# A two-layer SSD / RG-LRU trunk on one core: the order of the instructions taken from the scheduler's timeline model instead of its default model

## The chip, the cores and the metric

One core of a Trainium2 chip. The time is device microseconds (us) of one execution of the program. Five engines are spoken of: PE multiplies matrices, DVE and ACT work on vectors, POOL does so more slowly and reduces across partitions, SP issues loads and stores. Each engine runs its own list of instructions strictly in the order in which the compiled program has them, and waits at an instruction until what it needs is there.

## The reference

A step of a trunk of two layers runs over a new prompt (16 meta tokens and 1024 tokens) and over 8 running sequences of one new token each. All of it is float32:

```
for i in range(2):
    h = rms_norm(x, norm_mix_pre[i])
    m = ssd_mixer(h, ...) if i == 0 else rglru_mixer(h, ...)
    x = x + rms_norm(m, norm_mix_post[i])
    h = rms_norm(x, norm_ffn_pre[i])
    x = x + rms_norm(sq_relu_mlp(h, ffn_w1[i], ffn_w2[i]), norm_ffn_post[i])
```

The SSD mixer projects 1024 features to 6176, convolves over 4 tokens, and in chunks of 128 tokens computes for each of 8 groups of heads `scores = (C B^T) * L`, `y = scores x + (C h) * exp(cs)` and `h = h * exp(cs_end) + B^T (x * decay)`. The RG-LRU mixer has a gate, a convolution and a linear recurrence over the tokens. The MLP is `relu(x w1)^2 w2` with 4096 hidden features. Outputs are the new rows and the states of both mixers, for the prompt and for the running sequences.

## The kernel before

**Matrices.** Weights come in strips of 128 x 2048 float32, one MB each (`load_strip`, tile `ws`). A strip is scaled by a power of two and split in two float16 parts (`wconv`, `split`; tiles `wh` and, for the form with sums, `wp`), and every product is done in three passes of those parts. The power of two needs the largest magnitude of the strip: DVE or ACT takes it for each partition (`rm`), POOL's `partition_all_reduce` takes it over partitions (`wgb`, L265), and DVE works out the factors from `wgb` (`qw`, `pw`, `sw`, `winv`, in `strip_scale` and `pow2`). Where a `partition_all_reduce` stands among POOL's other work, the compiled program has a further POOL instruction (shown as `ISA` without operands) ahead of it and one behind it.

**Order of the program.** The mixer of layer 0 runs first (SSD: 8 groups, `ssd_group`), then its MLP (`ffn(0)`), then the RG-LRU mixer (`lru`) and `ffn(1)`. The source is written as lanes: generators that go one step on each `tick()`. Conversions of coming strips, sums of operands and normalisations are lanes beside the products. Beside the steps of an SSD group run the projections of the next one (`fill`).

**SSD group.** For each of 9 chunks PE transposes (`tp`) and multiplies (`cb`, `st`, `yo`); DVE forms `L`, `cbm`, `xdt`, `xdd`; the state is carried by POOL (`hst <- hst * ecd`, L1060) and then DVE (`hst <- hst + st`, L1061). Once per group POOL multiplies the 8 states of the running sequences (`h <- h * decfm`, 128 x 2048).

**MLP.** `ffn` goes through four blocks of 1024 hidden features. In blocks 1 to 3, and in the second products of blocks 0 to 2, the products are done as `unit`: seven products of quarters instead of eight, three units for a strip (the tokens lie in three chunks). A unit takes four of the eight PSUM tiles; ACT and DVE add its products up (`z`, `acc`). PE can therefore be at most two units ahead of DVE. A strip of these products needs, beside `wh`, the split quarters (`wp`, DVE's second part) and then four sums of quarters that POOL forms in the room of the strip (`ws <- ws`, in `sums`); only then does the next strip's `partition_all_reduce` come on POOL. Strips for w1 are called H strips here, those for w2 S strips. Ahead of block 1, POOL also forms the sums of the input (`input_sums`, tiles `f`).

**What sets the order.** Instructions go through `Queue` (L78), so almost all of them carry its lines: L89, or L92 where one has been pinned behind the one before. `hold` pins all engines to program order for the start of the kernel; activations that need a table stay in program order (`tab`). Everything else is put in order by the scheduler of the tile framework within what the data, the tiles' rooms and these pins allow. Its model of the machine is what `kernel()` gives to `TileContext` (L1655).

Of the kernel before, what the change touches and what calls it, by code (L numbers as in the profile page):

```python
# [17 lines left out]
DRAM = bass.MemoryType.DRAM  # L18
# [3 lines left out]
P = 128  # L22
D = 1024
KT = 8
# [3 lines left out]
T = 1050  # L28
# [25 lines left out]
def cols(c):  # L54
    """The columns of a chunk of tokens."""
    return slice(c * CW, c * CW + WC[c])


class Carve:
    """Small float32 tiles cut from larger ones."""  # L60
# [17 lines left out]
class Queue:  # L78
    """An engine; while hold is set its instructions are issued in program order, and later ones behind them."""
# [38 lines left out]
class Body:  # L118
# [7 lines left out]
    # ------------------------------------------------------- order of work  # L126
    def tick(self):
        """One step of every piece of work that runs beside the matrix products."""
        for lane in list(self.lanes):
            if next(lane, self) is self:  # L130
                self.lanes.remove(lane)
# [5 lines left out]
    def tab(self, *args, **kw):  # L137
        """An activation whose function needs a table set: these stay in program order."""
        if self.last_tab is None or self.nc.scalar.hold:
            self.last_tab = self.nc.scalar.activation(*args, **kw)  # L140
        else:
            with self.tc.issue_after(self.last_tab.ins):
                self.last_tab = self.nc.scalar.activation(*args, **kw)
# [8 lines left out]
    # ---------------------------------------------------------------- setup  # L152
    def setup(self):
# [8 lines left out]
        c = self.const  # L162
# [19 lines left out]
        # pre-norm gains and group-norm gains scaled by a power of two so that hi/lo fit float16  # L182
# [13 lines left out]
        # the inputs of the ffn leave room for sums of four  # L196
# [48 lines left out]
    def pow2(self, b, n, pool, tag):  # L245
        """p = the power of two at or below b; s = 2^14 / p."""
        nc = self.nc
        q = pool.tile([P, n], F32, tag="q" + tag, name="q" + tag)
        nc.vector.tensor_scalar(q, b, 1e-25, 1e25, op0=OP.max, op1=OP.min)
        p = pool.tile([P, n], F32, tag="p" + tag, name="p" + tag)  # L250
        nc.vector.tensor_scalar(p.bitcast(I32), q.bitcast(I32), EXPMASK, None, op0=OP.bitwise_and)
        s = pool.tile([P, n], F32, tag="s" + tag, name="s" + tag)
        nc.vector.tensor_scalar(s.bitcast(I32), p.bitcast(I32), -1.0, POW2SUM, op0=OP.mult, op1=OP.add)
        return s, p

    # -------------------------------------------------------------- weights
# [14 lines left out]
    def split(self, w, st, s, parts):  # L271
        """w = float16 hi and lo parts of st * s, s [P, parts] by contiguous column ranges."""
# [12 lines left out]
    def wconv(self, st, kind, cols=SW):  # L285
        """A strip of weights as float16 hi and lo parts [P, 2, KT, cols], the factor that undoes its scaling and,
        for kinds h and H, the factor of its hidden units. Kind a takes a bound from the sums of the magnitudes, kind s
        one that kind g found before; kinds 2 and S carry the factors of the hidden rows. Kinds H and S are for the
        products by Winograd's form: with the quarters that are used as they are."""
# [50 lines left out]
    def quarter(self, s, inv):  # L340
        """Scales that leave room for sums of four."""
# [7 lines left out]
    def sums(self, wp, st, s, npair, parts):  # L349
        """Steps: the quarters of a strip [K tiles, M] that are used as they are, A11, A12, A22 (A ij: m tile i, k  # L350
        tiles of parity j), as float16 parts in wp; then the sums of Winograd's form in the room of the strip. Only
        the first npair pairs of k tiles."""
# [20 lines left out]
    def product(self, ps, i, w, B, T, npair):  # L373
        """ps = one of the seven products of quarters over the first pairs of k tiles, three passes of the float16
        parts; open for the products of the other pairs where there are any."""
# [14 lines left out]
    def quadrant(self, w, B, npair, i, l):  # L390
        """The operands of m tile i by half l of the tokens over the other pairs."""
# [26 lines left out]
    def hidden_scale(self, wmax, inv):  # L418
        """The factors of one strip's hidden units: t = 2^7, or 2^6 where the squares are summed, / (power of two at or
        below the bound on the values before the square, the norm of the input times that of a column); returns  # L420
        t / (scales of the product); 1 / t^2 goes to rj."""
# [21 lines left out]
    def summed(self, b, s):  # L443
        """Whether the hidden units of a strip of block b enter the second product by Winograd's form."""
        return b < 3 and s < NSUM
# [6 lines left out]
    def bundle(self, ps, w, m, act, c, kts=range(KT), first=True, last=True):  # L452
        """ps += sum over k of w[k, m tile]^T act[k, chunk c], three passes of the float16 parts."""
# [14 lines left out]
    def new_u(self):  # L468
        """Float16 parts of the normed input by chunk and k tile."""
# [4 lines left out]
    def u_rows(self, U, c):  # L474
        """The bytes of chunk c of U as float32 rows."""
        return U[:, c].bitcast(F32).rearrange("p k s c -> p k (s c)")

    # ---------------------------------------------------------------- norms
    def rstd(self, sumsq, n, pool, w):
        """1 / sqrt(mean + eps) on every partition, from per-partition sums of squares."""  # L480
# [17 lines left out]
    def normed(self, x, ss, i, hi, lo, pool):  # L498
        """Steps: the pre-norm i of a chunk (its k tiles in x), as float16 parts in hi and lo [P, KT, n]."""
# [15 lines left out]
    def boundary(self, m, ss, xc, piece, ipost, xdst, ipre, U, pool):  # L515
        """Steps: x + norm(m) for a piece of a chunk to xdst; then its pre-norm."""
# [37 lines left out]
    def last_phase(self, ws, act, ipost, xsrc, xdst, ipre, evac, pre=None, split0=None):  # L554
        """The last product before a norm, chunk by chunk; the norms of a chunk run beside the next one."""
# [47 lines left out]
    def first_phase(self, strips, act, evac):  # L603
        """Products of the first strips after a norm: chunk 2 of the input comes last."""
# [15 lines left out]
    # ------------------------------------------------------------------ SSD  # L620
# [67 lines left out]
    def start_x(self, c):  # L688
        """A chunk of the input, in the room of later rows: its k tiles, and room left over."""
# [25 lines left out]
    def start_norm(self, U, c, x, sq, ufs):  # L715
        """Steps: the first pre-norm of a chunk."""
# [29 lines left out]
    def start(self, U):  # L746
        """The first pre-norm beside the first products, issued in this order."""
# [20 lines left out]
    def dt_phase(self, U, dts, dtt, w):  # L768
        """Step sizes, decays and their cumulative sums, tokens on partitions: columns (tile, head); tiles 0-7
        are the chunks of the prompt, 8 the meta tokens, 9 the sample tokens."""  # L770
# [31 lines left out]
        # the sums again, tokens along the rows, in DRAM, from where they are spread over the partitions  # L802
# [22 lines left out]
        # sample tokens  # L825
# [3 lines left out]
        # head rows by sample, then spread over the partitions of the features  # L829
# [13 lines left out]
    def softplus(self, out, x, pool, n, parts=1):  # L843
        """max(x, 0) + log1p(exp(-|x|)), the logarithm by the series of 2 artanh(e / (2 + e)); by parts of the
        columns that don't wait for each other."""
# [23 lines left out]
    def evac_ext(self, pre, ps, c, inv, bias=0.0):  # L869
        """A chunk of projected columns into the layout of the convolution: 8 x (3 state + 1), 3 zeros, tokens."""  # L870
# [10 lines left out]
    def conv_tile(self, pre, out, w4, b1, cvo):  # L881
        """Depthwise convolution of width 4; the last three columns of each sequence go to cvo [P, 27]."""
# [16 lines left out]
    def proj_x(self, g, start=False):  # L899
        """Projection and convolution of the x, B and C columns of a group."""  # L900
# [84 lines left out]
    def ssd_group(self, g):  # L985
# [26 lines left out]
        def spread(i):  # L1012
            """The cumulative sums of a chunk's tokens on every partition."""
# [68 lines left out]
        def sample_bc():  # L1082
            """B and C of the sample tokens, by way of DRAM, on every partition."""
# [22 lines left out]
        def sample_b(b2):  # L1106
            """Two sample tokens: h += x B and y = h C, B and C spread over the partitions."""
# [45 lines left out]
    def group_norm(self, g):  # L1153
        """Steps: gate, norm within the group, float16 parts."""
# [25 lines left out]
    def half_a(self):  # L1180
        """The first half of the output projection, kept in DRAM by chunks."""
# [43 lines left out]
    # ------------------------------------------------------------------ FFN  # L1225
    def ffn(self, l):
# [8 lines left out]
        for b in range(4):  # L1235
# [3 lines left out]
            def square(c, s, r):  # L1239
                """The squares of r (m tile, half of the tokens) as float16 parts, and their sums."""  # L1240
# [78 lines left out]
    def t_sums(self, f, t1, t234):  # L1319
        """Steps: the sums of quarters of the right operand for Winograd's form, in their room in f (B jl: k tiles of  # L1320
        parity j, half l of a chunk's tokens, the last half first): T1 = B12 - B11, T2 = B22 - T1, T3 = B22 - B12,
        T4 = B21 - T2, and their float16 parts."""
# [9 lines left out]
    def input_sums(self, U, TT, fp):  # L1332
        """Steps: the sums of quarters of the input, T1 in the room of B12 and the others in TT."""
# [16 lines left out]
    def unit(self, w, BT, c, npair, fp):  # L1350
        """Two m tiles by a chunk, [C12, C11, C22, C21] (C il: m tile i, half l of the tokens, the last half first), the
        first pairs of k tiles by Winograd's form: seven products of quarters."""
# [27 lines left out]
    # ------------------------------------------------------------------ LRU  # L1380
    def lru(self):
# [99 lines left out]
        # a bound on |h gate|: (32.3 max|x| + max|h0|) (norm of u times that of a column of weights + max|b|)  # L1481
# [74 lines left out]
def _strips(w, ns):  # L1556
    """[K, N] as [ns, 128, (K / 128) * (N / ns)], each strip contiguous per partition."""
# [4 lines left out]
def _fm(x):  # L1562
    """[..., n * 128] as [128, n, ...]"""
# [95 lines left out]
```

## Time and profile before

| | |
|---|---|
| runs of the kernel before | 2834.26, 2834.31 and 2837.87 us, median 2834.31 |
| span of the profiled execution | 2836.7 us |
| PE busy | 2583.1 us, 91% of the span |
| DVE, ACT, POOL busy | 2110.1, 1322.6, 691.4 us |
| instructions | 56933 |

No time beside its span is listed for the profiled execution; the span lies 2.4 us above the median of the runs and 1.2 us below the slowest.

The stages by the clock of the profile: the start to 71 us, the SSD groups to 852, the end of the mixer to 1065, the MLP of layer 0 to 1704, a boundary to 1846, the gates of the RG-LRU to 1988, its output to 2130, the MLP of layer 1 to 2769, the end to 2837. In a row of the timeline the first number is the start, the second the duration; the bracket at the end tells how long the engine had been idle and what ended that. Durations of neighbouring rows overlap by some 0.08 us, so that sums are taken from starts where that matters. "issue" in a bracket means that the engine waited for nothing that the profile shows.

### The profile page before, as it was taken

What the parts mean: (1) busy time and instruction counts of PE and PEld (TensorE: products, weight loads), DVE (VectorE), ACT (ScalarE), POOL (GpSimd) and SP (SyncE); (2) the same over time, 40 slices, a digit from 0 to 9 for tenths busy, and PEclk for the clock granted to TensorE, in tenths of its full rate; (3) what the DMA queues carried; (4) which work ended last, traced back from release to release, by engine and by line L of the source; (5) the groups of instructions that cost most, each with busy time, mean ns of one, the idle gap of its engine ahead of it and who ended that gap; (6) DMA issues with size and microseconds to landing.
All of it is one profiled execution on the core that took longest, in us unless ns stands there. A gap on an engine that the chain in (4) does not pass through costs nothing. (4 is left out here: it accounts for less than half of the span.)

```text
span 2836.7 us, 56933 instructions
## 1 busy us (share of the span) xinstructions
PE 2583.1 (91%) x23209; PEld 2060.6 (73%) x23209; DVE 2110.1 (74%) x5043; ACT 1322.6 (47%) x2148; POOL 691.4 (24%) x972
## 2 busy tenths in 40 slices
PE   4999999999999999789989999979999779989998
PEld 2666666666666667789989976646667779989976
DVE  4889778977873685568778788787685667878776
ACT  4655455545544354344253344658564335253352
POOL 2222111212212024442232201123014452231301
PEclk9999999999999999889999999989999989999999
DMA  3232233223345320101122123110220101111122
GB/s 123 99 119 90 87 107 115 102 88 108 113 159 187 117 106 31 46 31 46 61 72 79 46 110 113 63 62 33 89 108 31 46 31 46 47 45 53 54 73 95
DMA packets 52758, 229.15 MB, mean 81 GB/s; under 512 B 9056, under 2 KB 18416, under 8 KB 31632
## 3 DMA queue, kind: packets, MB, share of 16 engines
q1 hardware_dynamic: 46112, 190.81, 19.1%
q0 software_dynamic: 6384, 34.71, 3.1%
q8 instruction: 181, 2.97, 0.4%
q14 instruction: 81, 0.66, 0.1%
HBM read 186.28 MB, written 39.22 MB: 79 GB/s over the span
## 5 line engine op out<-in xcount | busy, mean ns | idle before, releaser
L89 PEld LDWEIGHTS <-wh 128*128 128x128 f16 x17040 | 1504.0, 99 | 503.7 <-issue 54.7
L89 PE MATMUL mm<-U,wh 128*128 128x350 f16 (+3 forms) x7056 | 989.4, 297 | 20.7 <-ACT rr L89 13.2
L89 PE MATMUL mm<-H,wh 128*128 128x175 f16 (+5 forms) x5664 | 557.7, 253 | 35.3 <-DVE z L89 30.4
L89 PEld LDWEIGHTS <-wp 128*128 128x128 f16 x3888 | 311.0, 99 | 87.6 <-issue 60.5
L89 POOL TENSOR_TENSOR ws<-ws 128x256 f32<-128x256 f32 (+1 forms) x192 | 205.2, 1069 | 328.6 <-DVE wp L89 214.4
L89 DVE TENSOR_TENSOR z<-z,mm 128x175 f32<-128x175 f32 (+3 forms) x648 | 228.4, 370 | 29.2 <-ACT z L89 22.0
L89 POOL PARTITION_ALL_REDUCE wgb<-rm x100 | 55.5, 555 | 656.6 <-issue 338.4
L89 PE MATMUL mm<-U,wp 128*128 128x175 f16 (+1 forms) x1728 | 154.8, 245 | 55.2 <-DVE z L89 55.1
L89 PE MATMUL mm<-TT,wh 128*128 128x175 f16 (+1 forms) x1728 | 167.0, 248 | 10.2 <-ACT TT L89 9.3
L89 ACT ACTIVATE z<-z,ti 128x700 f32<-128x700 f32 (+1 forms) x72 | 63.0, 875 | 183.5 <-DVE z L89 183.5
L89 DVE SCALAR_TENSOR_TENSOR wh<-ws,sw,wh 128x1024 f16<-128x1024 f32 x94 | 122.0, 1320 | 28.3 <-ACT wh L89 28.3
L89 DVE TENSOR_SCALAR qw<-wgb 128x1 f32<-128x1 f32 x103 | 15.5, 150 | 167.3 <-POOL wgb L89 167.1
L89 DVE SCALAR_TENSOR_TENSOR wh<-ws,s,wh 128x256 f16<-128x256 f32 x256 | 114.7, 490 | 11.1 <-ACT wh L89 11.1
L89 DVE TENSOR_REDUCE rm<-ws 128x1 f32<-128x2048 f32 x40 | 91.3, 2281 | 31.2 <-DMA ws<-w 26.7
L89 PE MATMUL mm<-H,wp 128*128 128x175 f16 (+1 forms) x864 | 90.5, 241 | 25.5 <-DVE z L89 23.1
L89 DVE TENSOR_TENSOR ss<-ss,sqt 128x350 f32<-128x350 f32 (+3 forms) x154 | 75.9, 500 | 41.8 <-ACT sqt L89 41.1
L89 ACT ACTIVATE wh<-ws,s 128x512 f16<-128x512 f32 x128 | 83.0, 710 | 48.0 <-POOL ws L89 23.2
L89 DVE SCALAR_TENSOR_TENSOR conv<-pre,ssmall,conv 128x1072 f32<-128x1072 f32 x78 | 103.8, 1330 | 0.1
L89 ACT ACTIVATE wh<-ws,sw 128x2048 f16<-128x2048 f32 x47 | 93.7, 1993 | 14.5 <-DVE sw L89 11.7
L89 DVE TENSOR_SCALAR L<-L,ncs 128x128 f32<-128x128 f32 (+1 forms) x288 | 90.6, 357 | 13.2 <-DMA L<-csd 13.2
L89 DVE TENSOR_TENSOR H<-z,H 128x175 f16<-128x175 f32 (+5 forms) x120 | 81.2, 694 | 23.6 <-ACT H L89 19.5
L89 ACT ACTIVATE pre<-mm,undo 128x8 f32<-128x8 f32 (+1 forms) x104 | 46.5, 474 | 110.7 <-PE mm L89 110.7
(279 smaller groups left out, 4176.9 us busy)
## 6 DMA issues: line engine op xcount, KB each, us to landing
ws<-w SPq DMA_DIRECT2D x64, 1024.0 KB, 4.9
ws<-w_ssd_in SPq DMA_DIRECT2D x24, 1024.0 KB, 5.4
L<-csd SPq DMA_DIRECT2D x64, 256.0 KB, 3.2
ws<-w_lru_in SPq DMA_DIRECT2D x12, 1024.0 KB, 4.9
xd<-xc POOLq DMA_DIRECT2D x6, 1400.0 KB, 5.5
xc<-xd SPq DMA_DIRECT2D x6, 1400.0 KB, 6.0
h<-ssd_h SPq DMA_DIRECT2D x8, 1024.0 KB, 4.9
bc<-bcd SPq DMA_DIRECT2D x8, 1024.0 KB, 4.8
```

Of the source, the lines that this page charges most:

```text
L89: r = f(*args, **kw)
```

## The change

One argument in `kernel()`; the rest of the diff takes comments and docstrings out, and no line number moves.

```
-    with _tile.TileContext(nc) as tc:
+    with _tile.TileContext(nc, schedule_with_timeline_sim=True) as tc:
         tile_trunk(tc, aps)
```

The scheduler puts the same instructions in another order. The counts on PE, DVE, ACT and SP are those of before; POOL has four of the operand-less `ISA` instructions fewer. PE's order is as before in the units of both MLPs; in the SSD groups projections of the next group stand ahead of steps that they stood behind. DVE's order differs by 30 to 100 places in the SSD groups and by three or four in the MLPs. Three places follow.

**Place 1, an H strip of the MLP.** DVE's rows between the last split of one strip (`wp_15764`) and the factors of the next one (`qw_16198`, from POOL's `wgb_16196`), in the kernel before:

```order
L89 SCALAR_TENSOR_TENSOR wp_15764<-ws_15397,sq4_15880,wp_15764 128x512
L89 TENSOR_TENSOR z_15368<-z_15368,mm_15367 128x175 x2
L89 SCALAR_TENSOR_TENSOR acc_10692<-z_15368,iq4_15229,acc_10692 128x700
L89 TENSOR_TENSOR z_15482<-z_15482,mm_15478 128x175
L89 TENSOR_REDUCE rm_16147<-ws_15761 128x1
L89 TENSOR_TENSOR z_15482<-mm_15479,z_15482 128x2x175
L89 TENSOR_TENSOR z_15482<-z_15482,mm_15479 128x175
L89 TENSOR_TENSOR z_15482<-z_15482,mm_15480 128x2x175
L89 TENSOR_TENSOR z_15482<-z_15482,mm_15481 128x175 x2
L89 SCALAR_TENSOR_TENSOR acc_10692<-z_15482,iq4_15229,acc_10692 128x700
L89 TENSOR_TENSOR z_15607<-z_15607,mm_15603 128x174
L89 TENSOR_SCALAR qw_16198<-wgb_16196 128x1
```

and in the changed kernel:

```order
L89 SCALAR_TENSOR_TENSOR wp_15764<-ws_15397,sq4_15880,wp_15764 128x512 x3
L89 TENSOR_TENSOR z_15368<-z_15368,mm_15364 128x175
L89 TENSOR_TENSOR z_15368<-mm_15365,z_15368 128x2x175
L89 TENSOR_TENSOR z_15368<-z_15368,mm_15365 128x175
L89 TENSOR_TENSOR z_15368<-z_15368,mm_15367 128x175
L89 TENSOR_REDUCE rm_16147<-ws_15761 128x1
L89 TENSOR_TENSOR z_15368<-z_15368,mm_15366 128x2x175
L89 TENSOR_TENSOR z_15368<-z_15368,mm_15367 128x175
L89 TENSOR_TENSOR z_15482<-z_15482,mm_15478 128x175
L89 TENSOR_SCALAR qw_16198<-wgb_16196 128x1
L89 TENSOR_SCALAR lb_16443<-wgb_16196,gb_103 128x1
L89 SCALAR_TENSOR_TENSOR acc_10692<-z_15368,iq4_15229,acc_10692 128x700
```

In the kernel before all of `z_15482`, the first row of `z_15607` and both `acc` rows stand ahead of `qw`; in the changed kernel only the seven rows of `z_15368` and `z_15482` that are shown and `rm` do, and both `acc` rows come behind it. The same place on POOL, before:

```order
L89 TENSOR_TENSOR ws_15397<-ws_15397 128x4x128 x4
L89 ISA
L89 ISA wgb_16196<-rm_16147 128x1
L89 ISA
L89 TENSOR_TENSOR ws_15761<-ws_15761 128x4x128 x4
```

and after:

```order
L89 TENSOR_TENSOR ws_15397<-ws_15397 128x4x128 x3
L89 ISA
L89 ISA wgb_16196<-rm_16147 128x1
L89 ISA
L89 TENSOR_TENSOR ws_15397<-ws_15397 128x4x128
L89 TENSOR_TENSOR ws_15761<-ws_15761 128x4x128 x3
```

One of the four sums of `ws_15397` has moved behind the `partition_all_reduce` of `wgb_16196`.

**Place 2, the state of an SSD group, on POOL.** The multiplications of `hst` by `ecd` are the states of successive chunks of one group; before:

```order
L89 ISA
L89 ISA wgb_5777<-rm_5734 128x1
L89 COPY cvo_5199<-pre_5202 128x3
L89 ISA
L89 TENSOR_TENSOR hst_5420<-hst_5346,ecd_957 128x256
L89 TENSOR_TENSOR gsq_5490<-gsq_5490,gsq_5491 128x350
L89 COPY cvo_5199<-pre_5448 128x24
L89 COPY pre_5701<-cst_5197 128x8x3
L89 MEMSET pre_5701 128x3
L89 TENSOR_TENSOR hst_5515<-hst_5420,ecd_957 128x256
L89 TENSOR_TENSOR hst_5589<-hst_5515,ecd_957 128x256
L89 TENSOR_TENSOR hst_5670<-hst_5589,ecd_957 128x256
```

and after, with the multiplication of the running sequences' states of the same stretch (`h0_6212`):

```order
L89 TENSOR_TENSOR h0_6212<-h0_6212,decfm_1046 128x2048
L89 TENSOR_TENSOR hst_5589<-hst_5515,ecd_957 128x256
L89 COPY pre_6243<-cst_6238 128x8x3
L89 MEMSET pre_6243 128x3
L89 ISA
L89 ISA wgb_6357<-rm_6276 128x1
L89 COPY pre_6489<-cst_6238 128x8x3
L89 MEMSET pre_6489 128x3
L89 ISA
L89 TENSOR_TENSOR hst_5670<-hst_5589,ecd_957 128x256
L89 COPY cvo_6240<-pre_6243 128x24
L89 TENSOR_TENSOR hst_5807<-hst_5670,ecd_957 128x256
```

The steps to `hst_5515`, `hst_5589` and `hst_5670` stood together, and now a `partition_all_reduce` with an `ISA` on either side stands between the last two.

**Place 3, the same stretch on DVE.** The rows ahead of the sum `hst_5670 + st_5655` in the kernel before:

```order
L89 SCALAR_TENSOR_TENSOR bc_5283,ys_5289<-h0_5171,bc_5283 128x128 x2
L89 TENSOR_TENSOR L_5495<-L_5495,cbm_5606 128x512
L89 SCALAR_TENSOR_TENSOR bc_5283,ys_5289<-h0_5171,bc_5283 128x128
L89 SCALAR_TENSOR_TENSOR yf_5170<-conv_4351,ssmall_81,cb_5652 128x128
L89 SCALAR_TENSOR_TENSOR yf_5170<-conv_4602,ssmall_81,cb_5652 128x128
L89 SCALAR_TENSOR_TENSOR conv_5643<-pre_5448,ssmall_81,conv_5643 128x1072
L89 TENSOR_TENSOR hst_5670<-hst_5670,st_5655 128x256
L89 SCALAR_TENSOR_TENSOR conv_5643<-pre_5448,ssmall_81,conv_5643 128x1072
L89 TENSOR_TENSOR yt_5671<-yo_5657,es_959 128x256
```

and in the changed kernel:

```order
L89 TENSOR_SCALAR L_5495<-L_5495,ncs_952 128x128 x4
L89 TENSOR_TENSOR L_5400<-L_5400,cbm_5532 128x512
L89 TENSOR_SCALAR qw_6359<-wgb_6357 128x1
L89 SCALAR_TENSOR_TENSOR conv_6019<-pre_5901,ssmall_81,conv_6019 128x1072
L89 TENSOR_SCALAR pw_6361<-qw_6359 128x1
L89 TENSOR_SCALAR sw_6363<-pw_6361 128x1
L89 TENSOR_SCALAR winv_6365<-pw_6361 128x1
L89 TENSOR_TENSOR undo_7070<-winv_6365,ginv_111 128x1
L89 SCALAR_TENSOR_TENSOR yf_5170<-conv_4351,ssmall_81,cb_5571 128x128
L89 SCALAR_TENSOR_TENSOR yf_5170<-conv_4602,ssmall_81,cb_5571 128x128
L89 TENSOR_TENSOR cbm_5606<-cb_5571,tri_88 128x128
L89 TENSOR_TENSOR hst_5670<-hst_5670,st_5655 128x256
```

The factors of a strip (`qw_6359` to `undo_7070`) and a convolution of the next group now stand between the rows of two chunks.

## The prediction

> **What bounds the kernel now.** I read the page first, then the busy time by stage, then the waits, and then the timeline of single stretches.
>
> ```profile
> span 2836.7 us, 56933 instructions
> PE 2583.1 (91%) x23209; PEld 2060.6 (73%) x23209; DVE 2110.1 (74%) x5043; ACT 1322.6 (47%) x2148; POOL 691.4 (24%) x972
> ```
>
> PE is busy for 2583.1 us, and nothing that an order can do goes below that. What is to be won or lost is its idle time, 253.6 us. The busy time by stage (after the bounds and the length: PE, weight loads, DVE, ACT, POOL, then granted clock) says where it lies:
>
> ```profile
> 71.00:852.00 781.00, 741.37 (x5134) 521.80 (x5132) 641.10 (x1760) 405.68 (x613) 166.95 (x277) 0.98 0.31 108
> ...
> 1065.00:1704.00 639.00, 573.37 (x6704) 539.55 (x6703) 467.79 (x1155) 259.32 (x454) 190.23 (x252) 0.95 0.16 58
> ...
> 1846.00:1988.00 142.00, 121.63 (x728) 80.41 (x726) 110.26 (x122) 98.53 (x128) 41.46 (x33) 0.93 0.12 42
> ...
> 2130.00:2769.00 639.00, 572.17 (x6729) 537.88 (x6727) 452.82 (x1134) 262.11 (x461) 191.16 (x254) 0.96 0.13 47
> ```
>
> The SSD groups leave PE idle for 39.6 us, each MLP for 66, the RG-LRU gates for 20.4. The waits name what PE waits for, and what that waits for in turn:
>
> ```profile
> POOL wgb L89 <- issue: 338.4, 56, 9.3
> ...
> DVE qw L89 <- POOL wgb L89: 167.1, 68, 11.7
> ...
> PE mm L89 <- DVE z L89: 113.2, 70, 6.2
> ```
>
> PE's largest wait is for DVE's `z`; DVE's largest is for POOL's `wgb`; and POOL stands idle ahead of `wgb` for 338.4 us in 56 places with nothing to wait for. One H strip of the MLP shows the chain, on DVE and on POOL:
>
> ```profile
> 1369.78 0.74 DVE L89 SCALAR_TENSOR_TENSOR wp<-ws,sq,wp 128x512 f16<-128x512 f32 x1
> ...
> 1373.08 2.29 DVE L89 TENSOR_REDUCE rm<-ws 128x1 f32<-128x2048 f32 x1 [0.21 <-DMA ws<-w]
> 1375.29 0.51 DVE L89 TENSOR_TENSOR z<-mm,z 128x350 f32<-128x350 f32 x1
> ...
> 1378.18 0.33 DVE L89 TENSOR_TENSOR z<-z,mm 128x174 f32<-128x174 f32 x1
> 1382.97 0.15 DVE L89 TENSOR_SCALAR qw<-wgb 128x1 f32<-128x1 f32 x1 [4.46 <-POOL wgb L89]
> ```
>
> ```profile
> 1370.62 5.85 POOL L89 TENSOR_TENSOR ws<-ws 128x512 f32<-128x512 f32 x4 [12.09 <-DVE wp L89]
> 1382.53 0.41 POOL L89 PARTITION_ALL_REDUCE wgb<-rm  x1 [6.06 <-issue]
> ```
>
> The last `wp` ends at 1370.5. POOL then takes 5.85 us for four sums, stands for 6.06, reduces in 0.41, and DVE's `qw` starts at 1382.97. Of these 12.4 us DVE fills 7.8 with work and waits for 4.46. The strip that follows:
>
> ```profile
> 1404.70 0.15 DVE L89 TENSOR_SCALAR qw<-wgb 128x1 f32<-128x1 f32 x1 [4.60 <-POOL wgb L89]
> ```
>
> ```profile
> 1383.00:1404.70 21.70, 21.09 (x277) 20.74 (x275) 16.90 (x41) 4.67 (x7) 6.03 (x5) 1.00 0.14 50
> ```
>
> A strip takes 21.7 us. PE is busy for 21.09 of them. DVE has 16.90 us of work and 4.6 us of waiting, 21.5 together: it has no more room than PE has. Where an order lengthens that one wait, DVE becomes the bound.
>
> **The change, part by part.** Work and counts stay; so each term is a wait that grows or shrinks. The sum is made against the span of 2836.7, and I carry the difference over to the median of 2834.3, since the profiled execution is only 2.4 us from it.
>
> *H strips of the MLPs (place 1).* One of four sums goes behind the reduction: the chain becomes 3/4 of 5.85, 4.4, plus 6.06, plus 0.41, 10.9 us. But of DVE's work only `rm` and seven `z` rows are left between `wp` and `qw`: `rm` 2.2, five narrow `z` at 0.33 less the overlap of 0.08, 1.25, two wide ones at 0.51 less 0.08, 0.86: 4.3 us, where 7.8 stood. DVE waits for 10.9 - 4.3 = 6.6 us in place of 4.5. The rows that went behind `qw` aren't saved, they come later. So DVE's strip is 16.9 + 6.6 = 23.5, over the 21.7 of now: 1.8 us. It is a closed loop (`wp`, sums, reduction, `qw`, the next `wp`), so that PE's lead over DVE of at most two units hides it once and not at each strip. I find the same shift at eight strips, two consecutive ones in each of two blocks in both MLPs: 8 x 1.8 = 14.4 us. The bounds: 0 where PE's lead covers a run of two (3.6 us), and 8 x 2.1 = 17 where nothing does.
>
> *S strips.* The same working gives waits that fall at some strips and rise at others, by 4 us at most either way. I take 0, and 6 us either way for the range.
>
> *The SSD groups (places 2 and 3).* Of a group's 94.5 us:
>
> ```profile
> 548.70:643.20 94.50, 89.75 (x610) 63.28 (x609) 77.84 (x214) 48.96 (x76) 20.62 (x36) 1.00 0.28 103
> ```
>
> PE idles for 4.75, DVE for 16.7. What a reduction costs on POOL beside the states is here:
>
> ```profile
> 513.77 0.62 POOL L89 TENSOR_TENSOR hst<-hst,ecd 128x256 f32<-128x256 f32 x1 [6.87 <-PE mm L89]
> ...
> 529.54 0.48 POOL L89 PARTITION_ALL_REDUCE wgb<-rm  x1 [6.22 <-issue]
> 537.05 0.91 POOL L89 TENSOR_TENSOR gsq<-gsq 128x348 f32<-128x348 f32 x1 [7.03 <-PE cb L89]
> ...
> 547.38 3.61 POOL L89 TENSOR_TENSOR h<-h,decfm 128x2048 f32<-128x2048 f32 x1
> 550.94 0.61 POOL L89 TENSOR_TENSOR hst<-hst,ecd 128x256 f32<-128x256 f32 x1
> ```
>
> It stands for 6.22 ahead of the reduction and for 7.03 behind it, whatever the profile puts the latter down to: the stretch of 6.87 ahead of 513.77 follows a reduction too, and has another releaser. In the changed order one lies between the multiplications to `hst_5589` and `hst_5670`: 6.22 + 0.48 + 7.03 + 0.61, 14.3 us, where they stood together. DVE has about 4 us of rows between its two sums (place 3):
>
> ```profile
> 542.67 1.32 DVE L89 SCALAR_TENSOR_TENSOR conv<-pre,ssmall,conv 128x1072 f32<-128x1072 f32 x1
> 543.92 0.34 DVE L89 SCALAR_TENSOR_TENSOR yf<-conv,ssmall,cb 128x128 f32<-128x128 f32 x1
> ...
> 547.59 3.48 DVE L89 TENSOR_SCALAR L<-L,ncs 128x128 f32<-128x128 f32 x1
> ...
> 551.32 0.52 DVE L89 TENSOR_SCALAR L<-L,ncs 128x128 f32<-128x128 f32 x2
> ...
> 552.80 0.69 DVE L89 TENSOR_TENSOR L<-L,cbm 128x512 f32<-128x512 f32 x1
> ```
>
> four `L` at 0.26, the product 0.69, the convolution 1.32, two `yf` at 0.34, the rest small. So DVE waits for up to 10 us there, less what it is late when POOL's part is done; half of it, 5, is my choice. DVE's 16.7 idle us per group have room for it, and PE's projections now stand ahead of the steps that wait. Against it stands PE's own idle time of 4.75 per group, part of which the fuller PE order can close. I set the one against the other: 0, with -38 (8 x 4.75, all idle time closed) and +42 (8 x 10 less 38) as bounds.
>
> A part of PE's idle time here has a cause of its own. Most rows of `L` take 0.28 us (shortest, median and longest in ns behind the colon), and some 3.7:
>
> ```profile
> L89 DVE TENSOR_SCALAR L<-L,ncs x288: 211/277/3718, 112.6 to 839.2; 128x128 f32<-128x128 f32 x128, 16x16 f32<-16x16 f32 x16
> ```
>
> The one at 547.59 took 3.48 and ended as POOL's multiplication of `h` ended (550.99), and PE stood idle for it:
>
> ```profile
> 551.54 0.67 PE L89 MATMUL yo<-hst,conv 128*128 128x256 f32 x2 [2.83 <-DVE yt L89]
> ```
>
> In the new order a convolution and a split `wh` stand beside that multiplication, and not `L`. By the `L` rows alone that would win 2.83 us in six groups that have it, 17 us. But two groups have other rows there:
>
> ```profile
> 185.68 3.65 DVE L89 TENSOR_TENSOR xds<-conv,dtfm 128x8 f32<-128x8 f32 x1
> ```
>
> ```profile
> 455.13 3.55 DVE L89 SCALAR_TENSOR_TENSOR yf<-conv,ssmall,ys 128x8 f32<-128x8 f32 x1
> ```
>
> Rows of 8 elements, held as long. So whatever stands there is held, and I take nothing for it. The Trainium skill ("GPSIMD Engine Reference", section "Key points") says that POOL shares its SBUF interfaces with DVE, in contention with instructions in a 2-port mode or with two SBUF inputs; a convolution and a split have two such inputs, so by it the 17 us aren't won either, and the two rows agree.
>
> *The rest.* The gates of the RG-LRU wait for ACT:
>
> ```profile
> 1864.24 1.19 PE L89 MATMUL mm<-xr,wab 128*128 128x268 f32 x2 [3.15 <-ACT Y L89]
> 1870.28 5.83 PE L89 MATMUL mm<-U,wh 128*128 128x350 f16 x24 [4.84 <-ACT rr L89]
> ```
>
> ACT's order moves a strip's split ahead of `Y` and a root behind it, in idle time of ACT: 0, or 5 us either way (one such gap). At the start of each MLP's sums POOL sets the pace:
>
> ```profile
> 1140.00:1235.00 95.00, 73.71 (x833) 71.17 (x831) 55.20 (x138) 30.93 (x51) 47.28 (x65) 0.86 0.10 36
> ```
>
> Neither PE nor DVE is full there; the order moves reductions among POOL's rows without taking one away: 0, or 5 us either way. Start, boundaries and end are nearly as before: 0.
>
> The sum is 14.4 us: 2834.3 + 14.4 = 2849.
>
> **The rivals.** *Faster.* The projections that stand ahead in PE's order give DVE a longer lead in each SSD group, and PE's idle time of 4.75 us per group closes: -38, with 14 from the MLPs 2834 - 24 = 2810. It decides if DVE's wait for `hst` stays under what PE has queued ahead. For it: PE's gaps in this stage are single ones of some 3 us; against it: DVE's new waits and the held rows.
>
> *No change.* PE's lead covers the runs of two strips, and what the SSD groups win and lose cancels: 2834. For it: the lower bound of the H strips; against it: PE is full there only as long as DVE is on time.
>
> *Much slower.* The waits for `hst` aren't hidden: 42 in the SSD groups and 14 in the MLPs, 2890. For it: DVE is in order, and everything PE needs stands behind the waiting row. The clock adds to it where gaps are long:
>
> ```profile
> 552.00:556.00 4.00, 4.00 (x29) 3.03 (x28) 4.00 (x9) 3.97 (x7) 0.00 (x0) 1.00 0.06 18
> ...
> 1252.00:1258.00 6.00, 0.23 (x4) 0.09 (x2) 2.83 (x7) 3.31 (x7) 3.25 (x7) 0.90 0.42 164
> 1258.00:1262.00 4.00, 3.96 (x28) 3.95 (x28) 2.77 (x7) 0.84 (x2) 2.95 (x5) 0.50 0.01 2
> ```
>
> After the gap of 2.83 us at 548.7 the granted clock stayed at 1.00; after one of almost 6 us it was 0.50 for 4 us, which is 2 us more. The 1.8 us of an H strip cost no clock by that; a bare wait of 10 us would. The Trainium skill ("TensorE: Matmul & The Clock Gate", section "What's actually happening") puts the border at about 3.4 us of idle time; both rows agree with it.
>
> **How the numbers follow.** A difference within 0.2%, 5.7 us, is about what a measurement can't tell from none. Forecast (H strips as worked out, the rest about even) 0.43; faster 0.28; no change 0.17; much slower 0.12. Slower is then 0.55. The range goes from the faster rival, 2810, to the much slower one, 2890.
>
> **What would show it.** Right: the wait of DVE's `qw` at the strips of place 1 is 6 to 7 us, their period 23 to 24, and PE's waits for `z` in the MLP stages grow by some 7 us each; DVE waits for POOL's `hst` by 5 us or so per group, with the SSD stage still about 781 us long. Wrong: the strips stay at 21.7 us, or the SSD stage moves by more than 15 us either way; a `L` beside `h` with no row held for 3.5 us would refute the held rows.

## The result, and the profile after

The changed kernel takes 3095.45 us, median of four runs from 3094.7 to 3103.17; the kernel before has 2836.09 in the same count of runs. The ratio is 1.0916, with a 95% interval from 1.0901 to 1.0932: 9% slower, 259 us, where 15 us were forecast and the range ended at 2890. The page of the changed kernel has the same work and more idle time:

```profile
span 3093.1 us, 56896 instructions
...
PE 2643.5 (85%) x23209; PEld 2104.6 (68%) x23209; DVE 2106.5 (68%) x5043; ACT 1315.3 (43%) x2148; POOL 710.2 (23%) x972
```

Of the span's 256.4 us more, 60.4 are PE's own busy time with the same 23209 matmuls (2643.5 less 2583.1), and 196 are idle time of PE (449.6 less 253.6). The mean granted clock fell from 0.968 to 0.940. Some of the waits that grew most, as the list of waits has them:

```profile
DVE qw L89 <- POOL wgb L89: 255.7, 74, 11.7
...
PE mm L89 <- DVE z L89: 190.3, 82, 7.7
...
ACT wh L89 <- POOL ws L89: 145.1, 11, 17.0
ACT Bt L89 <- DVE xdd L89: 143.7, 53, 10.0
...
DVE hst L89 <- POOL hst L89: 83.9, 23, 11.8
```

The first two stood at 167.1 and 113.2. The third, ACT waiting for POOL's sums before it can split a strip, stood at 75.1, and the fourth, ACT waiting for DVE's `xdd` in the SSD groups, at 22.9. The last one, DVE waiting for the state in the SSD groups, was 13.6 in the kernel before:

```profile
DVE hst L89 <- POOL hst L89: 13.6, 19, 1.2
```

To compare stages, I take the same landmarks in every trace, from the start of the first to the start of the last: the products into `st` (the SSD groups), the products with `H` as an operand (each MLP but its first part), and those with `xr` (the RG-LRU gates). The busy time between them, for the groups and the two MLPs, in the kernel before:

```profile
127.30:834.50 707.20, 673.12 (x4498) 475.38 (x4497) 582.64 (x1642) 356.43 (x550) 145.13 (x247) 0.98 0.31 110
1094.60:1756.70 662.10, 596.29 (x6849) 554.21 (x6848) 499.33 (x1207) 268.39 (x467) 182.15 (x240) 0.96 0.17 62
...
2166.90:2824.80 657.90, 591.07 (x7040) 559.94 (x7037) 469.90 (x1168) 252.22 (x449) 187.51 (x242) 0.96 0.15 53
```

and in the changed kernel:

```profile
136.10:932.70 796.60, 691.96 (x4436) 488.56 (x4436) 582.15 (x1647) 360.84 (x550) 161.18 (x252) 0.93 0.29 99
1208.60:1921.90 713.30, 602.46 (x6847) 561.50 (x6845) 497.37 (x1195) 261.61 (x459) 193.09 (x244) 0.94 0.16 55
...
2367.70:3081.50 713.80, 604.67 (x7040) 573.14 (x7037) 472.50 (x1160) 252.24 (x453) 196.82 (x243) 0.94 0.14 49
```

The groups lose 89.4 us, the MLPs 51.2 and 55.9; together 196.5 of 256.4. The rest lies in the gates (122.1 to 138.4), in the stretches between, and 9 us ahead of the first state. DVE has the same busy time in each of these stages within 3 us. POOL is busy for 9 to 16 us more in each, far less than it stands idle. PE, with about the same matmuls, is busy for longer, at a lower granted clock in each of them.

**An H strip.** The strip from 1534.6 to 1560.6 takes 26.0 us, not 21.7, and not the 23.5 of the prediction. DVE, then POOL, then ACT:

```profile
1534.62 0.15 DVE L89 TENSOR_SCALAR qw<-wgb 128x1 f32<-128x1 f32 x1 [5.11 <-POOL wgb L89]
...
1544.98 2.48 DVE L89 SCALAR_TENSOR_TENSOR wh<-ws,sq,wh 128x1024 f16<-128x1024 f32 x2 [3.28 <-ACT wh L89]
...
1560.59 0.15 DVE L89 TENSOR_SCALAR qw<-wgb 128x1 f32<-128x1 f32 x1 [4.52 <-POOL wgb L89]
```

```profile
1534.17 0.41 POOL L89 PARTITION_ALL_REDUCE wgb<-rm  x1 [5.95 <-issue]
1541.65 1.26 POOL L89 TENSOR_TENSOR ws<-ws 128x512 f32<-128x512 f32 x1 [7.06 <-issue]
1550.38 3.97 POOL L89 TENSOR_TENSOR ws<-ws 128x512 f32<-128x512 f32 x3 [7.47 <-DVE wp L89]
```

```profile
1542.94 2.00 ACT L89 ACTIVATE wh<-ws,sq 128x2048 f16<-128x2048 f32 x1 [17.03 <-POOL ws L89]
```

The one sum that went behind the reduction (place 1 on POOL) starts 7.06 us after it and ends at 1542.91. ACT has stood idle for 17 us when it splits the strip at 1542.94, and this sum is what it waited for; DVE waits for ACT, and only then do the next strip's `wp` come. The same holds at the eight strips that the prediction had counted: ACT's split waits for that sum, after 15 to 17 us of idle time, and from one `qw` to the next they take 25.9 to 26.4 us, where the same strips took 20.7 to 21.8 before. That is 38 us in all.

**An SSD group.** Around place 2 in the group from 530.4 to 637.6, which takes 107.2 us between products that lay 94.2 us apart before: POOL, DVE, PE and the clock there.

```profile
592.15 0.51 POOL L89 PARTITION_ALL_REDUCE wgb<-rm  x1 [5.95 <-issue]
...
602.95 0.60 POOL L89 TENSOR_TENSOR hst<-hst,ecd 128x256 f32<-128x256 f32 x1 [7.76 <-issue]
```

```profile
603.59 0.42 DVE L89 TENSOR_TENSOR hst<-hst,st 128x256 f32<-128x256 f32 x1 [7.49 <-POOL hst L89]
...
604.53 2.47 DVE L89 SCALAR_TENSOR_TENSOR wh<-ws,sw,wh 128x1024 f16<-128x1024 f32 x2
...
607.58 0.41 DVE L89 TENSOR_TENSOR xdd<-tp,dtd 128x256 f32<-128x256 f32 x1
```

```profile
595.17 7.00 PE L89 MATMUL mm<-U,wh 128*128 128x350 f16 x46
608.36 1.22 PE L89 MATMUL st<-xdd,Bt 128*128 128x256 f32 x2 [6.19 <-ACT Bt L89]
```

```profile
601.00:608.30 7.30, 1.17 (x8) 0.55 (x6) 4.71 (x9) 0.27 (x1) 0.76 (x2) 0.77 0.07 9
608.30:612.00 3.70, 3.64 (x14) 3.17 (x15) 1.88 (x6) 2.46 (x6) 0.62 (x1) 0.53 0.66 270
612.00:616.00 4.00, 4.00 (x28) 2.79 (x28) 3.63 (x10) 0.62 (x2) 0.00 (x0) 1.00 0.23 66
```

DVE waits for the state for 7.49 us. PE's projections that had been put ahead cover 7.0 us, then it stands for 6.19 us, and for 3.7 us after that its clock is granted at 0.53. What PE waits for at the end is the next `Bt`, which ACT makes behind DVE's `xdd`, and `xdd` stands on DVE behind the late state and behind a strip's split of 2.47 us.

### The profile page after: what moved, and what is told of

It is laid out like the page before. It is cut to its first block, busy times and chain, and to the rows that moved or that the text cites. A ratio compares the mean times of both kernels' runs of the same rounds, so it can differ in the third digit from the quotient of the medians.

```text
span 3093.1 us, 56896 instructions
## 1 busy us (share of the span) xinstructions
PE 2643.5 (85%) x23209; PEld 2104.6 (68%) x23209; DVE 2106.5 (68%) x5043; ACT 1315.3 (43%) x2148; POOL 710.2 (23%) x972
## 4 chain that ended last, share of the span: by engine, by line
PE 34%; DVE 28%; issue 19%; DMA 7%; ACT 7%; POOL 5%; SPq 0%; POOLq 0%; DVEq 0%; ACTq 0%
PE mm L89 27%; DVE wh L89 6%; DMA ws<-w 5%; DVE z L89 4%; DVE rm L89 2%; PE yo L89 2%; PE mm L92 2%; DVE r L89 2%; ACT wh L89 2%; POOL f L89 1%; DVE conv L89 1%; DVE H L89 1%; DVE L L89 1%; DVE wp L89 1%; POOL ws L89 1%
## 5 line engine op out<-in xcount | busy, mean ns | idle before, releaser
L89 PEld LDWEIGHTS <-wh 128*128 128x128 f16 x17040 | 1527.6, 100 | 621.2 <-DVE z L89 92.0
L89 PE MATMUL mm<-U,wh 128*128 128x350 f16 (+3 forms) x7056 | 1014.6, 301 | 102.4 <-DVE z L89 41.4
L89 PE MATMUL mm<-H,wh 128*128 128x175 f16 (+5 forms) x5664 | 566.2, 256 | 63.5 <-DVE z L89 39.8
L89 PE MATMUL mm<-H,wp 128*128 128x175 f16 (+1 forms) x864 | 91.8, 244 | 32.2 <-DVE z L89 32.1
L89 POOL TENSOR_TENSOR hst<-hst,ecd 128x256 f32<-128x256 f32 x64 | 46.1, 720 | 263.5 <-PE yo L89 118.7
L89 ACT ACTIVATE wh<-ws,sq 128x2048 f16<-128x2048 f32 x24 | 47.8, 1994 | 135.7 <-POOL ws L89 135.7
L89 PE MATMUL st<-xdd,Bt 128*128 128x256 f32 (+1 forms) x144 | 51.4, 442 | 54.7 <-ACT Bt L89 49.0
```

The costliest lines, as they stand in the source:

```text
L89: r = f(*args, **kw)
```

## The experiments

Theory A says that it is the reductions: POOL stands for some 6 us ahead of a `partition_all_reduce` and some 7 behind it, and the new order has rows there that others wait for. Theory B says that the new order of DVE, ACT and PE loses by itself. The forecasts of single runs give these two names a narrower sense in places. Times are of one run each, unless an interval is given; the kernel before took 2831 to 2839 us beside them. The stages, by the landmarks above, in us:

| | groups | MLP 0 | gates | MLP 1 | span |
|---|---|---|---|---|---|
| before | 707.2 | 662.1 | 122.1 | 657.9 | 2836.7 |
| changed | 796.6 | 713.3 | 138.4 | 713.8 | 3093.1 |
| e1 changed, POOL as before | 868.6 | 676.6 | 123.7 | 677.9 | 3092.4 |
| e2 before, POOL as changed | 780.0 | 709.6 | 125.0 | 710.5 | 3017.5 |
| e6 changed, DVE as before | 838.7 | 731.0 | 124.1 | 728.8 | 3129.6 |
| e7 changed, DVE and POOL as before | 827.9 | 685.0 | 124.7 | 683.6 | 3035.4 |
| e5 changed, sums first | 793.6 | 702.0 | 138.0 | 702.2 | 3062.5 |
| e12 changed, SSD strips by copy | 702.7 | 710.5 | 138.2 | 715.4 | 2985.2 |
| e8 order of changed, copies | 705.7 | 567.4 | 117.3 | 563.8 | 2643.9 |
| e9 order of before, copies | 696.6 | 582.6 | 116.0 | 579.6 | 2647.5 |
| e3 before, other reduction | 693.8 | 604.2 | 116.7 | 594.9 | 2692.5 |
| e4 changed, other reduction | 702.5 | 572.0 | 117.4 | 565.7 | 2661.4 |

**One engine's order at a time (e1, e2, e6, e7).** The instructions of an engine are chained in the order of a table, taken from the other kernel's program; the scheduler puts the rest in a new order around that, which is neither kernel's. In the traces of these four runs the pinned engines have the order that they were to have, instruction by instruction.

```
     with _tile.TileContext(nc, schedule_with_timeline_sim=True) as tc:
         tile_trunk(tc, aps)
+        pin(tc)
...
+        for a, b in zip(seq, seq[1:]):
+            tc.add_manual_dep(b, a.name, mybir.DependencyInfo(mybir.DependencyClass.NoSync,
+                                                              mybir.DependencyReason.DATA), reason="pin")
```

> The changed kernel, with POOL alone pinned to the order that it has in the kernel before; the scheduler with the timeline model orders the other engines around that. Theory A (it is where the reductions stand among POOL's rows, each with some 6 us of idle time ahead and 7 behind, that makes the loss): most of the 257 us of the span goes, at or below 2920 us. Theory B (the order of DVE, ACT and PE makes the loss by itself: rows that PE waits for stand behind others that wait): at or above 3030 us.

Measured: 3094.16 us, no gain at all, where theory B had it (3030 or more). The MLPs win 36 us each, and the groups lose 72 more.

> The kernel before, with POOL alone pinned to the order of the changed kernel; the default scheduler orders the other engines around that. Theory A: most of the loss appears, at or above 3000 us. Theory B: at or below 2900 us.

Measured: 3019.24 us, where theory A had it (3000 or more). POOL's new order brings 181 us of loss, in the groups and in the MLPs, with the default scheduler for all other engines.

> The changed kernel with DVE alone pinned to the order of the kernel before. Theory A1 (one engine's order carries the loss, and it is DVE's, which waits most for POOL): at or below 2920 us. Theory A2 (any order that leaves no room for the reductions' idle time loses, whichever engine it is on; POOL's own order of before changed nothing): at or above 2980 us.

Measured: 3131.32 us, slower than the changed kernel, as A2 has it.

> The changed kernel with DVE and POOL both pinned to the order of the kernel before; PE, ACT and SP are ordered by the timeline model around them. If the loss lies in how DVE's and POOL's rows stand to each other, it is gone but for a rest: 2830 to 2900 us. If ACT's or PE's order carries a part by itself, it stays above 2950 us.

Measured: 3037.09 us. Even with the two engines of the chain as before, 200 us of loss stay, most of it in the groups (827.9 against 707.2), where the timeline model puts PE's and ACT's rows. Neither POOL's nor DVE's order, put back alone or together, takes the loss away (PE's and ACT's were not put back alone), and A in its narrow form, that POOL's order alone does it, has fallen with e1. What is left is a broader A, any order made with no room for the reductions' idle time loses to them, or B.

**The reduction without its idle time (e3, e4, and timed as e10, e11).** In place of the one instruction:

```
-        nc.gpsimd.partition_all_reduce(gb, gmax, P, RED.absmax)
+        g1 = ty.tile([1, 1], F32, tag="g1", name="g1")
+        nc.gpsimd.tensor_reduce(g1, gmax, axis=AX.C, op=OP.max)
+        one = self.rowp.tile([1, 1], F32, tag="one", name="one")
+        nc.sync.dma_start(one, g1)
+        nc.sync.dma_start(gb, one.to_broadcast([P, 1]))
```

> The kernel before, the partition_all_reduce of each weight strip replaced by a partition-axis tensor_reduce on POOL to one element and two small transfers that spread it over the partitions. If the idle time of some 13 us around a reduction comes with that one kind of instruction, it is gone here. Both theories: 2760 to 2840 us, as PE's waits for z in the MLPs behind that chain (113 us in all) shrink, unless the two transfers (an estimate of 4 us from the 4.9 us that a load of a strip takes to land) take as long as what they replace.

> The same replacement in the changed kernel. Theory A: with no idle time around the reductions their place hardly matters, so it is within 80 us of the run before it. Theory B: it stays 180 us or more above the run before it.

Measured: 2694.28 us in the kernel before and 2663.18 us in the changed one. The idle time is gone with that kind of instruction; between two sums of a strip POOL now reduces like this (e10, the changed kernel again):

```profile
1306.54 3.98 POOL L89 TENSOR_TENSOR ws<-ws 128x512 f32<-128x512 f32 x3 [14.56 <-DVE wp L89]
1310.87 0.31 POOL L89 CROSS_LANE_REDUCE g<-rm 128x1 f32<-128x1 f32 x1 [0.35 <-DVE rm L89]
1311.15 1.26 POOL L89 TENSOR_TENSOR ws<-ws 128x512 f32<-128x512 f32 x1
```

The very form of place 1, three sums, the reduction, the fourth sum: 0.6 us now lie between the third and the fourth, where 13.4 lay in the strip above (5.95, 0.41 and 7.06). Theory B, which had e4 180 us or more above e3, has fallen: e4 lies below it. I had expected 2760 to 2840 us of e3; it came out below.

> The timeline model's order with the maximum over partitions taken without partition_all_reduce, timed against the kernel before. By its first look (2663 us) the ratio to the kernel before is 0.938; it holds if the run is repeatable to 0.3%.

> The default scheduler's order with the maximum over partitions taken without partition_all_reduce, timed against the kernel before: 2694 us by its first look, a ratio of 0.949. The timeline model's order is then the better one of the two by 31 us, if both intervals are under 10 us wide.

Measured: 2656.59 us, ratio 0.938 with a 95% interval from 0.9364 to 0.9397, and 2690.3 us, ratio 0.9506, from 0.9492 to 0.952. The intervals are apart: without the `partition_all_reduce`, the timeline model's order is the better one, by about 34 us. Both compute everything, and e10 is the fastest version of the study that does. In its profile DVE waits for `wgb` still, now for the transfer:

```profile
DVE qw L89 <- DMA wgb<-one: 127.7, 64, 11.6
```

**The same two orders, instruction by instruction (e8, e9).** e3 and e4 were scheduled anew, so their orders aren't those of the two kernels. Here each engine is pinned to the very order of its kernel, and one instruction is another:

```
-        nc.gpsimd.partition_all_reduce(gb, gmax, P, RED.absmax)
+        nc.gpsimd.tensor_copy(gb, gmax)
```

> The changed kernel with every engine pinned to the very order of the changed kernel, and each strip's partition_all_reduce replaced by a copy of one element per partition on POOL, at the same place. What it leaves out is the maximum over partitions. Theory A (the order is good by itself and loses by the 13 us or so that a partition_all_reduce keeps POOL from its next row): 2640 to 2760 us, 330 us or more below the changed kernel. Theory B (the order loses by itself): above 2950 us, since only DVE's waits for wgb (256 us, of which PE sees a part) get shorter.

> The same for the kernel before: every engine pinned to its very order, the partition_all_reduce of each strip replaced by a copy. Theory A: 2650 to 2760 us, and no more than 60 us from the run before it either way. Theory B: 150 us or more below the run before it.

Measured: 2645.6 us and 2649.22 us. In both traces every engine has the very order of its kernel. The order that loses 259 us with the reductions is level with the other one without them. Its page (e8) and its MLP stages:

```profile
PE 2531.5 (96%) x23209; PEld 2033.0 (77%) x23209; DVE 2112.4 (80%) x5043; ACT 1320.4 (50%) x2148; POOL 719.2 (27%) x972
```

```profile
1090.50:1657.90 567.40, 564.25 (x6847) 532.79 (x6845) 490.94 (x1179) 258.26 (x450) 189.32 (x240) 1.00 0.19 70
2068.50:2632.30 563.80, 563.80 (x7040) 543.09 (x7037) 469.47 (x1156) 249.66 (x446) 196.18 (x241) 1.00 0.17 60
```

PE is busy for all but 3 us of both MLPs, at a clock of 1.00. So the reductions with their idle time cost the order of before 2836.7 - 2647.5 = 189 us (182 against the kernel before as timed beside e9), and the new one 3093.1 - 2643.9 = 449 us. That is the broader A, and B has no share in the loss that this can show. The orders of e1, e2, e6 and e7 were not run without the reductions; that their losses hang on them as well is not shown.

**Two of the places by themselves (e5, e12).** e5 pins each reduction behind the sums of the strip before:

```
-        nc.gpsimd.partition_all_reduce(gb, gmax, P, RED.absmax)
+        if self.last_sum is None:
+            nc.gpsimd.partition_all_reduce(gb, gmax, P, RED.absmax)
+        else:
+            with self.tc.issue_after(self.last_sum.ins):
+                nc.gpsimd.partition_all_reduce(gb, gmax, P, RED.absmax)
...
-            tt(o, a, b, op=op)
+            self.last_sum = tt(o, a, b, op=op)
```

> The changed kernel; each strip's reduction is pinned behind the last of the four sums of the strip before it, and nothing else is pinned. Theory A (the reduction with its 6 us ahead and 7 us behind delays whatever stands next to it): the sum that stood behind the reduction no longer holds up the split of its strip, the H strips go from 26 us to 23.5, and the two MLP stages (713 us each) shorten by 20 us or more each: at or below 3055 us. Theory B (the loss is DVE's wait for qw, as the prediction had it): the chain gets longer by one sum, 1.5 us for each of some 16 H strips, and the time rises to 3095 to 3120 us.

Measured: 3064.2 us, some 30 less, between the forecasts of A (at or below 3055) and B (3095 to 3120). DVE's rows of the same strip:

```profile
1533.19 0.15 DVE L89 TENSOR_SCALAR qw<-wgb 128x1 f32<-128x1 f32 x1 [4.93 <-POOL wgb L89]
...
1538.96 2.47 DVE L89 SCALAR_TENSOR_TENSOR wh<-ws,sq,wh 128x1024 f16<-128x1024 f32 x2
...
1556.03 0.15 DVE L89 TENSOR_SCALAR qw<-wgb 128x1 f32<-128x1 f32 x1 [5.90 <-POOL wgb L89]
```

The split no longer waits, and the strip takes 22.8 us in place of 26.0. A was right on the place and near on the strip (23.5), and too high on the stages: 11 us less each, not 20. The eight strips alone win 25 us in the two MLPs; others lose some of it again. What the MLPs still lose against the kernel before, 40 and 44 us, lies in good part elsewhere. In the first MLP 15 us of it are at its start: three strips there, from one `qw` to the next, took 25.6, 32.1 and 21.5 us in the kernel before, 33.1, 33.1 and 31.0 in the changed one and 31.0, 32.6 and 30.7 here. Which rows make them longer was not followed.

e12 has the very order of the changed kernel on all engines, and a copy only for the SSD mixer's strips (`if kind == "a"`).

> The changed kernel with every engine pinned to its very order; only the strips of the SSD mixer (projections in but for the first two, and out) have their partition_all_reduce replaced by a copy, which leaves out the maximum over partitions for them; the MLPs and the RG-LRU keep theirs. Theory A (in the SSD groups too it is the reductions beside the state's steps): the groups, from the first to the last product of a state, go from 797 us to 720 or less, DVE's waits for POOL's hst from 84 us to under 20, and the MLP stages stay at 713 us: 2950 to 3010 us in all. Theory B (there PE's order runs into ACT and DVE by itself): the groups stay above 760 us.

Measured: 2987.4 us. The groups are back at 702.7 us, the MLPs as they were, and DVE's wait for the state is all but gone:

```profile
DVE hst L89 <- POOL hst L89: 3.2, 3, 1.5
```

So the 89 us of the groups come from their strips' reductions too, and not from PE's or ACT's order by itself. How the scheduler's model accounts for a `partition_all_reduce` is not shown by any run; that its order reads as if POOL were free soon after one is my reading of places 1 and 2.

## Why the prediction was wrong, point by point

**What bounds the kernel: right on POOL's idle time, and not followed far enough.** The chain named (PE waits for `z`, DVE for `wgb`, POOL idle around the reduction) is the one of the MLPs. In the SSD groups the same idle time acts through the state: DVE's wait for `hst` rose from 13.6 to 83.9 us. I worked from the chain strip by strip and missed that the total at stake was 189 us in the kernel before and could more than double. The floor was wrong too: PE's 2583.1 us can fall. In e9 the same matmuls in the same order are busy for 2525.2 us, at a mean granted clock of 0.990 in place of 0.968. Whether an order alone can bring that, no run shows.

**H strips: the step that failed is "One of four sums goes behind the reduction: the chain becomes 3/4 of 5.85, 4.4, plus 6.06, plus 0.41, 10.9 us".** It books that sum as 1.5 us won and has nobody wait for it. In the trace it starts 7.06 us after the reduction, and ACT's split of the strip, DVE's second part and the next `wp` wait for it. The wait of DVE for `qw` was 5.1 and 4.5 us, not 6.6. The strip was 26.0, not 23.5: to DVE's 16.8 us of work and 4.5 for `qw` come 3.3 of waiting for ACT, 0.8 for a load and some short gaps, which my sum didn't have. Over the eight strips the difference to the kernel before is 38 us, where the term was 14.4. With all four sums put ahead (e5) the wait for ACT is gone and the strip is 22.8; that this is close to my 23.5 is chance, since the sum was made for another form. I had followed the chain to `qw` and not asked who else waits for the row that was moved past an idle stretch of 7 us which I had quoted myself.

**S strips and the start of the MLPs, taken at 0, 5 or 6 either way: wrong in size.** The MLPs lose 51 and 56 us; e5 wins back 11 each, and some 40 each remain, which e8 shows to hang on the reductions. I took "the order moves reductions among POOL's rows without taking one away" for no change; but the loss came with reductions that were neither more nor fewer: what counts is what stands behind them. Which rows those are here stays open.

**SSD groups, taken at 0: the mechanism right, its cover wrong.** The prediction had DVE wait for the state by up to 10 us at place 2, with 5 chosen, and had PE's projections cover it. DVE waited for 7.5 at the place shown and for 84 in all eight groups, some 10 each. PE's cover of 7.0 us ran out, since behind the late state DVE still had some 4 us of rows before the one that PE needed; PE then stood for 6.2 us. The bound of +42 was too low as well: 89. It was built on DVE's waits less all of PE's former idle time, as if the one could use the other up; the two places looked at lie apart in the group, the former gap beside POOL's `h`, the new one behind a reduction.

**The held rows: right.** The row of `L` is held in two groups of the changed kernel, in place of six, and in five others something else is, beside the multiplication of `h`. At 372.18 it was a factor of one element per partition:

```profile
372.18 3.56 DVE L89 TENSOR_TENSOR undo<-winv,ginv 128x1 f32<-128x1 f32 x1
```

In the eighth DVE had no row there. The convolution named in the prediction is the held row in one group, a split `wh` in none. So the 17 us weren't to be had.

**The clock: too small.** I had said that a strip's 1.8 us costs no clock. PE's busy time rose by 60 us, nearly a quarter of the loss: the idle stretch of 6.2 us at 602 to 608 is followed by 3.7 us at about half of the clock. With bare waits of 6 to 17 us in the chain I should have counted such stretches. The border of about 3.4 us that the Trainium skill gives ("TensorE: Matmul & The Clock Gate", section "What's actually happening") fits this place. It is no sharp one in these traces, as the prediction's two rows made it seem: in the kernel before, a gap of 2.68 us, from 643.2 to 645.9, has these rows around and behind it, with a granted clock of 0.85 and 0.72:

```profile
643.00:647.00 4.00, 1.32 (x5) 0.77 (x4) 4.00 (x8) 0.78 (x2) 2.91 (x2) 0.85 0.00 0
647.00:651.00 4.00, 4.00 (x24) 2.98 (x23) 4.00 (x8) 3.52 (x6) 0.00 (x0) 0.72 0.02 4
```

**The rival "much slower"** was the one that came: DVE in order, and what PE needs behind the waiting row. Its price of 56 us was about a fifth of the loss. My chance of 0.55 for slower was on the right side, and for a reason that held in part: the H strips got longer, if by another wait. But they carry 38 of the 256 us; most of the loss lies where the forecast had a 0. The size came from adding single local waits, each at its smallest plausible length, and from setting gains on PE against losses on DVE.

## What to carry to other kernels

When an order changes, list for every long instruction or idle stretch of an in-order engine (here some 6 us ahead of most of 111 reductions and 7 behind) which rows stand behind it now, and follow each of them to everyone who waits, not only the chain that was critical before. The whole cost of such a stretch is measured by taking it away with the order pinned: 189 us here in the kernel before, and a new order made it 449. The better move than another order was to take the long thing away: the same reduction in another instruction is worth 5 to 6%, and only with that does the timeline model's order win.

## What the runs showed of the hardware

A `partition_all_reduce` of 128 values takes POOL 0.41 us (median of 111 in the kernel before, the longest 2.0), and with the operand-less instructions around it some 6 us more ahead and 7 behind where it stands among POOL's other work. A `tensor_reduce` over the partition axis of the same 128 values takes 0.31 us (median of 109 in e10, the longest 2.1), with no idle time of that kind around it in the rows shown.

POOL's multiplication of 128 x 2048 (3.6 us) held up one DVE row until its own end in all eight groups of the kernel before and in seven of the changed one, whatever that row was: `L`, a product, a convolution, or rows with 1 and 8 elements per partition. The held rows lasted 3.3 to 4.5 us. A row that began just ahead of it wasn't held: at 370.93 in the changed kernel a convolution took its usual 1.33 us, and the multiplication, from 370.98, took 4.75 us.
